# Moved loads, shorter transposes and grouped products in a two-layer trunk kernel

## The chip, the cores and the metric

The kernel runs on one core of a Trainium2 chip. The metric is the device time of one execution in microseconds (us); shown is the median of several runs. The core has TensorE (matrix products; its queue also holds the weight loads), VectorE, ScalarE, GpSimd and SyncE, which run side by side and wait for each other through semaphores. In the profile they are PE, PEld (weight loads), DVE, ACT, POOL and SP; SPq, ACTq and POOLq are the queues that issue DMA transfers.

## The reference

One sequence of 512 tokens of width 1024 passes two layers. Each layer has a token mixer, a cross attention to 256 memory vectors, and a feed-forward block with a short convolution; all sums go into the residual `h`. Layer 0 mixes with GLA and RWKV-7, layer 1 with RG-LRU and mLSTM.

```
mem_n = rms_norm(mem, mem_norm_g)
h = x
for layer in range(DEPTH):
    xn = rms_norm(h, norm_mix_g[layer])
    ...                      # layer 0: gla_group, rwkv7_group; layer 1: rglru_group, mlstm_group
    h = h + mixed @ w_mix_out[layer]
    h = h + memory_cross_attention(rms_norm(h, norm_xattn_g[layer]), mem_n, ...)
    h = h + conv_glu_ffn(rms_norm(h, norm_ffn_g[layer]), ...)
return rms_norm(h, final_norm_g)
```

GLA and RWKV-7 carry a state from chunk to chunk (64 tokens in the kernel): per chunk a state update from keys and values, and an output that reads the state before the chunk. Cross attention is a softmax over the 256 memory vectors in four heads.

## The kernel before

Activations lie transposed: eight tiles of 128 features x 512 tokens. A dense product is made of three TensorE products per 128 x 128 block: weights and activations are each split into a rounded part (`hi`, made on ScalarE) and the rest (`lo`, made on VectorE), and `hi*hi`, `hi*lo` and `lo*hi` are summed in PSUM. `wload` loads one block of weights on SP's queue into a ring of three raw tiles and splits it into a ring of two; `block` and `half` call it. PSUM has eight banks: a ring `mm` of three for dense products and a ring `ax` of five for all else. The pool `qr` has 16 tiles of 512 columns that serve many short-lived values.

The Tile framework orders the instructions: it goes by the order in which they are written and by what it reckons to be ready, so work written later fills gaps of work written earlier. On each engine that order is then fixed; an instruction that waits holds up all behind it on its engine. `issue_after(x)` puts instructions behind `x` on its engine. Products into one PSUM tile keep their written order.

The stages, with their times in the profile below:
- start (to 20 us): the constructor `Trunk` loads vectors and constants (`cmat`: identity, block ones, a mask) and runs ten small products on ones as warm-up; `trunk` loads the eight tiles of x and the first weights; the first loop in `gla` multiplies each x tile with the gate's low-rank weights (two products) and with the keys' weights (three).
- GLA (to about 88 us): projections, transposes, masked scores, then for two pairs of heads the sums `u` of keys and values of seven chunks and the state `S` from them, and the outputs.
- RWKV's four pairs (to about 232 us): per pair p the projections r, k, v, decays, v transposed into `SV`, products within chunks, and a bonus term that reads v last. `during(p)` puts GLA's gates and the memory's norm among them.
- RWKV's solve and scan (to about 340 us): a triangular inverse on VectorE, then eight chunks, each with products into `w`, `yp`, `z`, `uu` and again `yp`, for four pairs and two heads e of a pair. The two heads use different halves of the partitions; `SV[0]` is completed by VectorE, `SV[1]` by ScalarE. The products of the memory's keys and values (`memory_k`, `memory_v`), written later, run between.
- Cross attention: per head two halves of 256 tokens: scores, softmax `e`, transposes into `pT`, then values.
- Feed-forward, layer 1, and the end: the last block of `ffn` is done in two halves of 256 tokens, and `finish` adds, norms, scales and stores each half.

The state sums of GLA before, with one PSUM tile for two chunks each, written and read in turn:

```
for c in range(7):
    if c % 4 < 2:
        us[c // 4, c % 2] = K.ax.tile([P, 2, P], F32, name="ax")
    u = us[c // 4, c % 2][:, (c % 4) // 2]
```

Of the kernel before, what the change touches and what calls it, by code (L numbers as in the profile page):

```python
# [8 lines left out]
F32 = mybir.dt.float32  # L9
# [3 lines left out]
ALU = mybir.AluOpType  # L13
# [4 lines left out]
P = 128  # L18
# [124 lines left out]
class Trunk:  # L143
    def __init__(self, ctx, tc, I):
# [14 lines left out]
        nc.gpsimd.dma_start(out=self.cm, in_=I["cmat"][:, 0:384])  # L159
# [10 lines left out]
        for i in range(10):  # L170
            self.mmul(warm[:, 0:P], self.ones["d"], self.ones["d"])
# [6 lines left out]
        nc.vector.tensor_scalar(out=self.bo64m, in0=self.bo64, scalar1=1.0 / 64.0, scalar2=None, op0=ALU.mult)  # L178
# [61 lines left out]
    def wload(self, src, kb, m):  # L240
# [4 lines left out]
        n = kb * m  # L245
        self.last_load = nc.sync.dma_start(out=raw[:, :n], in_=src.rearrange("p k m -> p (k m)"))
        self.act(hi[:, :n], raw[:, :n], AF.Copy)
        self.tt(lo[:, :n], raw[:, :n], hi[:, :n].bitcast(F32), ALU.subtract)
        sh = lambda t: t[:, :n].rearrange("p (k m) -> p k m", m=m)
# [149 lines left out]
def xattn(K, l, nm, kd, vd, h, feed):  # L399
    nc, X = K.nc, nm.X  # L400
    with ExitStack() as es:
# [25 lines left out]
        def heads(hd, q):  # L427
            pT = [K.ax.tile([P, T], F32, name="ax") for _ in range(2)]
            for half in range(2):
# [18 lines left out]
                for i in range(2):  # L448
# [3 lines left out]
                    for m in range(2):  # L452
                        nc.tensor.transpose(pT[m][:, t * P:(t + 1) * P], e[:, i, m * P:(m + 1) * P], K.ident)  # L453
# [30 lines left out]
def memory_norm(K, sm):  # L484
# [5 lines left out]
    for i in range(4):  # L490
        f = K.qr.tile([P, T], F32, name="xs")
        nc.sync.dma_start(out=pair(f), in_=src[:, 2 * i:2 * i + 2])
        M.append(f)
        sq = K.qr.tile([P, T], F32, name="xs") if i else acc
# [7 lines left out]
    r = K.qr.tile([P, T], F32, name="xs")[:, 0:256]  # L502
# [90 lines left out]
def gla(K, nm, wga, wk, squares, after, Y):  # L593
    nc, X = K.nc, nm.X
    with ExitStack() as es:
# [5 lines left out]
        with K.tc.issue_after(after.ins):  # L601
            nc.vector.tensor_copy(out=gm, in_=gf)
        wa = gp.tile([48, 256], F32, name="walpha")
# [96 lines left out]
        for p in range(2):  # L700
            us = {}
            for c in range(7):
                if c % 4 < 2:
                    us[c // 4, c % 2] = K.ax.tile([P, 2, P], F32, name="ax")
                u = us[c // 4, c % 2][:, (c % 4) // 2]
                r = slice(64 * (c % 2), 64 * (c % 2) + 64)
                for e in range(2):
                    hd = 2 * p + e
                    K.mmul(u[64 * e:64 * e + 64], kt[p][r, c // 2, 64 * e:64 * e + 64],
                           v[r, c // 2, hd * P:(hd + 1) * P])  # L710
                if c == 0:
# [55 lines left out]
def rwkv(K, X, Y, during, after):  # L767
# [3 lines left out]
    with ExitStack() as core:  # L771
# [12 lines left out]
        with ExitStack() as es:  # L784
# [13 lines left out]
            vp = wt.tile([P, 640], F32, name="vp")  # L798
            nc.gpsimd.memset(vp, 0.0)
            for p in range(4):  # L800
                r = shifted(K, new(), K.block("w_rw", p, X), p, om)
                k = shifted(K, new(), K.block("w_rw", 4 + p, X), 4 + p, om)
                v = shifted(K, vp[:, 64:576], K.block("w_rw", 8 + p, X), 8 + p, om)
# [28 lines left out]
                for w0, w1 in ((0, 4), (4, 8), (8, 9)):  # L832
# [406 lines left out]
def trunk(tc, I, out):  # L1239
    nc = tc.nc  # L1240
    with ExitStack() as ctx:
        K = Trunk(ctx, tc, I)
        sm = K.pool(ctx, "nsm", 1)
        with ExitStack() as es:
# [8 lines left out]
            for k in range(1, KD):  # L1253
                load(k)
# [113 lines left out]
```

## Time and profile before

| | us |
|---|---|
| median of 3 runs (1559.96 to 1565.53) | 1561.15 |
| the profiled execution | 1558.83 |
| its span, first to last instruction | 1557.0 |
| TensorE busy in the span | 1527.6 |
| VectorE busy | 914.9 |
| ScalarE busy | 683.7 |
| GpSimd busy | 23.3 |

The span is what the profile shows; about 1.8 us of the execution lie outside it. Busy times say how much of the span an engine worked; an engine that is off the path loses nothing by idling. A product's duration includes its way through the array, so products overlap: the pace is read from one start to the next, not from durations.

### The profile page before, as it was taken

What the parts mean: (1) busy time and instruction counts of PE and PEld (TensorE: products, weight loads), DVE (VectorE), ACT (ScalarE), POOL (GpSimd) and SP (SyncE); (2) the same over time, 40 slices, a digit from 0 to 9 for tenths busy, and PEclk for the clock granted to TensorE, in tenths of its full rate; (3) what the DMA queues carried; (4) which work ended last, traced back from release to release, by engine and by line L of the source; (5) the groups of instructions that cost most, each with busy time, mean ns of one, the idle gap of its engine ahead of it and who ended that gap; (6) DMA issues with size and microseconds to landing.
All of it is one profiled execution on the core that took longest, in us unless ns stands there. A gap on an engine that the chain in (4) does not pass through costs nothing.

```text
span 1557.0 us, 20187 instructions
## 1 busy us (share of the span) xinstructions
PE 1527.6 (98%) x8077; PEld 1240.3 (80%) x8077; DVE 914.9 (59%) x1348; ACT 683.7 (44%) x1101; POOL 23.3 (1%) x62
## 2 busy tenths in 40 slices
PE   8999999999999999999999999999999999999997
PEld 6876777787888888888888878788888888888886
DVE  7537679645655755556633386777557556565333
ACT  5465563345444543333332267566345333333221
POOL 2000000001000000000000000000000000000000
PEclk9999999999999999999999999999999999999999
DMA  4222226226331333332233321224213333322332
GB/s 165 81 75 82 68 62 192 90 93 224 111 106 48 107 97 98 99 95 95 92 98 102 94 98 49 75 73 149 72 51 117 105 98 95 96 95 89 101 98 78
DMA packets 50175, 152.19 MB, mean 98 GB/s; under 512 B 5505, under 2 KB 8865, under 8 KB 50081
## 3 DMA queue, kind: packets, MB, share of 16 engines
q1 hardware_dynamic: 45664, 142.87, 29.2%
q10 hardware_dynamic: 3536, 5.38, 1.0%
q0 software_dynamic: 880, 2.66, 0.4%
q8 instruction: 63, 1.03, 0.3%
q14 instruction: 32, 0.25, 0.1%
HBM read 144.59 MB, written 6.29 MB: 97 GB/s over the span
## 4 chain that ended last, share of the span: by engine, by line
PE 89%; DVE 6%; ACT 3%; DMA 1%; issue 1%; SPq 0%; DVEq 0%; ACTq 0%
PE mm L209 77%; PE ax L209 10%; DVE wl L194 1%; ACT e L206 1%; PE ax L453 1%; ACT wh L206 1%; DVE tm L194 1%; DVE bb L892 0%; DVE tu L194 0%; DMA raw<-in_w_kv 0%; DMA raw<-in_w_gla 0%; DVE au L881 0%; DVE e L814 0%; ACT a L206 0%; DVE stk L203 0%
## 5 line engine op out<-in xcount | busy, mean ns | idle before, releaser
L209 PE MATMUL mm<-xs,wh 128*128 128x512 f32 (+1 forms) x3627 | 1110.4, 387 | 2.4 <-DVE vp L203 1.8
L209 PEld LDWEIGHTS mm<-xs,wh 128*128 128x128 f32 x3627 | 671.8, 188 | 147.9 <-issue 8.0
L209 PE MATMUL mm<-xs,wl 128*128 128x512 f32 (+1 forms) x1814 | 700.3, 386 | 0.6 <-DVE wl L194 0.5
L206 ACT ACTIVATE wh<-raw 128x1024 fp32r<-128x1024 f32 (+2 forms) x273 | 264.8, 970 | 528.5 <-PE mm L209 412.1
L194 DVE TENSOR_TENSOR wl<-raw,wh 128x1024 fp32r<-128x1024 f32 (+2 forms) x272 | 302.6, 1113 | 211.8 <-ACT wh L206 210.8
L209 PEld LDWEIGHTS mm<-xs,wl 128*128 128x128 f32 x1814 | 341.0, 188 | 71.9 <-issue 1.8
L194 DVE TENSOR_TENSOR upad<-mm,rstd 128x512 f32<-128x512 f32 (+1 forms) x52 | 35.9, 690 | 95.5 <-PE mm L209 95.3
L194 DVE TENSOR_TENSOR h<-h,mm 128x512 f32<-128x512 f32 (+1 forms) x73 | 49.5, 677 | 69.3 <-PE mm L209 69.1
L194 DVE TENSOR_TENSOR g<-mm,rstd 128x512 f32<-128x512 f32 (+1 forms) x44 | 30.4, 692 | 76.0 <-PE mm L209 75.9
L203 DVE SCALAR_TENSOR_TENSOR c<-upad,vec,c 128x512 f32<-128x512 f32 (+1 forms) x88 | 65.9, 749 | 3.3 <-ACT c L206 1.8
L209 PE MATMUL mm<-wh,xs 128*128 128x256 f32 (+1 forms) x256 | 66.4, 349 | 0.0
L206 ACT ACTIVATE c<-c 128x512 f32<-128x512 f32 (+1 forms) x44 | 27.8, 632 | 87.1 <-DVE c L203 87.1
L209 PEld LDWEIGHTS mm<-wh,xs 128*128 128x128 f32 x256 | 44.8, 194 | 6.3 <-issue 1.0
L209 PE MATMUL mm<-wl,xs 128*128 128x256 f32 (+1 forms) x128 | 45.3, 354 | 3.8 <-DVE wl L194 3.8
L206 ACT ACTIVATE xs<-g 128x512 fp32r<-128x512 f32 (+1 forms) x44 | 27.8, 633 | 26.9 <-DVE g L194 26.9
L206 ACT ACTIVATE c<-upad,vec 128x512 f32<-128x512 f32 (+1 forms) x44 | 35.3, 802 | 1.5 <-DVE upad L194 1.5
L206 ACT ACTIVATE e<-ax,mx,scl 128x256 f32<-128x256 f32 x32 | 17.8, 560 | 39.8 <-DVE mx L194 39.8
L194 DVE TENSOR_TENSOR g<-c,g 128x512 f32<-128x512 f32 (+1 forms) x44 | 30.4, 692 | 5.8 <-ACT c L206 1.4
L194 DVE TENSOR_TENSOR nacc<-nacc,nsq 128x512 f32<-128x512 f32 x45 | 32.8, 730 | 0.3
L203 DVE SCALAR_TENSOR_TENSOR xs<-h,vec,xs 128x512 fp32r<-128x512 f32 x40 | 29.9, 749 | 3.5 <-ACT xs L206 3.4
L194 DVE TENSOR_TENSOR xs<-ax,xs 128x512 fp32r<-128x512 f32 x32 | 21.3, 687 | 18.0 <-ACT xs L206 18.0
L206 ACT ACTIVATE xs<-h,vec 128x512 fp32r<-128x512 f32 x40 | 28.8, 719 | 6.5 <-DVE h L194 6.5
(353 smaller groups left out, 1221.9 us busy)
## 6 DMA issues: line engine op xcount, KB each, us to landing
raw<-in_w_up SPq DMA_DIRECT2D x86, 512.0 KB, 3.4
raw<-in_w_dn SPq DMA_DIRECT2D x32, 512.0 KB, 3.4
raw<-in_w_kk SPq DMA_DIRECT2D x16, 512.0 KB, 3.6
raw<-in_w_kv SPq DMA_DIRECT2D x16, 512.0 KB, 3.9
raw<-in_w_q SPq DMA_DIRECT2D x16, 512.0 KB, 3.6
raw<-in_w_o SPq DMA_DIRECT2D x32, 256.0 KB, 2.6
raw<-in_w_cd SPq DMA_DIRECT2D x16, 512.0 KB, 3.2
raw<-in_w_rw SPq DMA_DIRECT2D x14, 512.0 KB, 3.6
```

The costliest lines, as they stand in the source:

```text
L194: (eng or self.nc.vector).tensor_tensor(out=out, in0=a, in1=b, op=op)
L203: return self.nc.vector.scalar_tensor_tensor(out=out, in0=a, scalar=s, in1=b, op0=op0, op1=op1)
L206: return self.nc.scalar.activation(out=out, in_=a, func=f, **kw)
L209: self.last_mm = self.nc.tensor.matmul(out, lhsT=l, rhs=r, start=start, stop=stop)
L453: nc.tensor.transpose(pT[m][:, t * P:(t + 1) * P], e[:, i, m * P:(m + 1) * P], K.ident)
```

## The change

- Start: the constants are loaded on SP's queue behind all x tiles (before: first on GpSimd's queue), and the scaled block of ones made from them is computed later. `wload` can load and split a block in parts; the first block goes in two halves, with loads of x between. 16 warm-up products for 10.
- Attention: all eight transposes of a head follow its second half; `pT` is allocated there.
- The memory's norm loads on GpSimd's queue, and its squares lie in a one-buffer tile of RWKV's pool, not in `qr`.
- GLA: the sums of four chunks share a PSUM tile (one full bank); all products of a pair are written ahead of the first read.
- RWKV: v is a `qr` tile of its own without padding, with four transposes into one PSUM tile in place of nine in three.
- RWKV's scan: `w`, `uu` and the second products of `yp` are written with e=1 first, and the rest of each group is put behind its first product.
- End: the gain of the last norm is multiplied into `h[j]`, j < 7, on ScalarE ahead of time; `finish` then multiplies three blocks at once and stores 3 + 3 + 2 blocks.

```diff
@@ class Trunk
-        nc.gpsimd.dma_start(out=self.cm, in_=I["cmat"][:, 0:384])
...
-        for i in range(10):
+        for i in range(16):
             self.mmul(warm[:, 0:P], self.ones["d"], self.ones["d"])
...
-        nc.vector.tensor_scalar(out=self.bo64m, in0=self.bo64, scalar1=1.0 / 64.0, scalar2=None, op0=ALU.mult)
...
-    def wload(self, src, kb, m):
+    def wload(self, src, kb, m, parts=1, between=None):
...
+        n = kb * m // parts
+        src = src.rearrange("p k m -> p (k m)")
+        for i in range(parts):
+            s = slice(i * n, (i + 1) * n)
+            self.last_load = nc.sync.dma_start(out=raw[:, s], in_=src[:, s])
+            if between:
+                between(i)
+        for i in range(parts):
+            s = slice(i * n, (i + 1) * n)
+            self.act(hi[:, s], raw[:, s], AF.Copy)
+            self.tt(lo[:, s], raw[:, s], hi[:, s].bitcast(F32), ALU.subtract)
@@ xattn, heads
-            pT = [K.ax.tile([P, T], F32, name="ax") for _ in range(2)]
+            es = []
             for half in range(2):
...
-                    for m in range(2):
-                        nc.tensor.transpose(pT[m][:, t * P:(t + 1) * P], e[:, i, m * P:(m + 1) * P], K.ident)
+                    es.append(e[:, i])
+            pT = [K.ax.tile([P, T], F32, name="ax") for _ in range(2)]
+            for m in range(2):
+                for t in range(4):
+                    nc.tensor.transpose(pT[m][:, t * P:(t + 1) * P], es[t][:, m * P:(m + 1) * P], K.ident)
@@ memory_norm
-        nc.sync.dma_start(out=pair(f), in_=src[:, 2 * i:2 * i + 2])
+        nc.gpsimd.dma_start(out=pair(f), in_=src[:, 2 * i:2 * i + 2])
         M.append(f)
-        sq = K.qr.tile([P, T], F32, name="xs") if i else acc
+        sq = tmp.tile([P, T], F32, name="msq") if i else acc
...
-    r = K.qr.tile([P, T], F32, name="xs")[:, 0:256]
+    r = tmp.tile([P, T], F32, name="msq")[:, 0:256]
@@ gla
             nc.vector.tensor_copy(out=gm, in_=gf)
+            nc.vector.tensor_scalar(out=K.bo64m, in0=K.bo64, scalar1=1.0 / 64.0, scalar2=None, op0=ALU.mult)
...
-            us = {}
+            us = [K.ax.tile([P, 4, P], F32, name="ax") for _ in range(2)]
             for c in range(7):
-                if c % 4 < 2:
-                    us[c // 4, c % 2] = K.ax.tile([P, 2, P], F32, name="ax")
-                u = us[c // 4, c % 2][:, (c % 4) // 2]
+                u = us[c % 2][:, c // 2]
...
+            for c in range(7):
+                u = us[c % 2][:, c // 2]
                 if c == 0:
                     K.act(S[:, p, 0], u, AF.Copy)
@@ rwkv
-            vp = wt.tile([P, 640], F32, name="vp")
-            nc.gpsimd.memset(vp, 0.0)
...
-                v = shifted(K, vp[:, 64:576], K.block("w_rw", 8 + p, X), 8 + p, om)
+                v = shifted(K, new(), K.block("w_rw", 8 + p, X), 8 + p, om)
...
-                for w0, w1 in ((0, 4), (4, 8), (8, 9)):
-                    ps = K.ax.tile([P, 4, P], F32, name="ax")
-                    for w in range(w0, w1):
-                        nc.tensor.transpose(ps[:, w - w0], vp[:, w * 64:w * 64 + P], K.ident)
-                    if w0 < 8:
-                        K.act(SV[0][64:128, w0:w1, p], ps[64:128, :, 0:64], AF.Copy)
-                    w = max(w0, 1)
-                    K.act(SV[1][0:64, w - 1:w1 - 1, p], ps[0:64, w - w0:w1 - w0, 64:128], AF.Copy)
+                ps = K.ax.tile([P, 4, P], F32, name="ax")
+                for t in range(4):
+                    nc.tensor.transpose(ps[:, t], v[:, t * P:(t + 1) * P], K.ident)
+                for e in range(2):
+                    for i in range(2):
+                        K.act(SV[e][R[1 - e], i::2, p], ps[R[i], :, R[e]], AF.Copy)
...
-                during(p)
+                during(p, wt)
...
+            def group(products):
+                products[0]()
+                with K.tc.issue_after(K.last_mm.ins):
+                    for f in products[1:]:
+                        f()
...
-                for p in range(4):
-                    for e in range(2):
-                        K.mmul(w[R[e], p], stk[e][:, p, c, 0:64], SV[e][:, c, p])
+                group([lambda e=e, p=p: K.mmul(w[R[e], p], stk[e][:, p, c, 0:64], SV[e][:, c, p])
+                       for p in range(4) for e in (1, 0)])
...
+                    group([lambda e=e, p=p: K.mmul(uu[R[e], p], BKT[:, p, c, R[e]], SV[e][:, c, p])
+                           for p in range(4) for e in (1, 0)])
...
+                group([lambda e=e, p=p: K.mmul(yp[R[e], p], SV[e][R[e], c, p], BB[R[e], p, c, 64:128], False, p == 3)
+                       for p in range(4) for e in (1, 0)])
@@ trunk
-            wk = K.wload(I["w_gla"][:, 2], KD, P)
-            for k in range(1, KD):
+            rest = iter(range(1, KD))
+            wk = K.wload(I["w_gla"][:, 2], KD, P, 2, lambda i: load(next(rest)))
+            for k in rest:
                 load(k)
+            nc.sync.dma_start(out=K.cm, in_=I["cmat"][:, 0:384])
...
-        def during(p):
+        def during(p, tmp):
...
-                    for j in range(KD):
-                        K.stt(h[j][:, s], h[j][:, s], K.v("final_norm_g", j), r, ALU.mult, ALU.mult)
-                        if j % 2:
-                            (nc.sync, nc.scalar)[j // 2 % 2].dma_start(out=dst[:, j - 1:j + 1, s],
-                                                                      in_=ht[:, j - 1:j + 1, s])
+                    rb = r.rearrange("p (o m) -> p o m", o=1)
+                    for a, b in ((0, 3), (3, 6), (6, 8)):
+                        c = min(b, KD - 1)
+                        K.mul(ht[:, a:c, s], ht[:, a:c, s], rb.to_broadcast([P, c - a, 256]))
+                        if b > c:
+                            K.stt(h[c][:, s], h[c][:, s], K.v("final_norm_g", c), r, ALU.mult, ALU.mult)
+                        (nc.scalar if a == 3 else nc.sync).dma_start(out=dst[:, a:b, s], in_=ht[:, a:b, s])
+
+                def feed(j, t):
+                    nm.feed(j, t)
+                    K.act(t, t, AF.Copy, scale=K.v("final_norm_g", j))
```

## Rows read from the trace of the kernel before

**Rows 1.** The page's busy times; a piece of the chain of waits (start, length, what)

```profile
PE 1527.6 (98%) x8077; PEld 1240.3 (80%) x8077; DVE 914.9 (59%) x1348; ACT 683.7 (44%) x1101; POOL 23.3 (1%) x62
372.81 62.39 PE mm L209 x274
```

**Rows 2.** Windows of TensorE: stretch, length, busy (instructions), granted clock, DMA share, GB/s

```profile
0.00:20.00 20.00, 15.07 (x57) 0.91 0.74 261
300.00:320.00 20.00, 20.00 (x281) 1.00 0.34 105
```

**Rows 3.** Start: timeline, chain, one window (PE, PEld, DVE, ACT, POOL; third-last: clock)

```profile
2.23 4.64 PE L209 MATMUL mm<-ones_d 128*128 128x128 f32 x20 [2.23 <-POOL ones_d L166]
1.66 7.04 DMA raw<-in_w_gla
11.10 0.80 PE L209 MATMUL mm<-xs,wl 128*128 128x512 f32 x1 [0.52 <-DVE wl L194]
12.00:13.00 1.00, 1.00 (x4) 0.55 (x3) 1.00 (x3) 1.00 (x3) 0.00 (x0) 0.50 1.03 420
20.63 0.39 PE L209 MATMUL mm<-xs,wl 128*128 128x512 f32 x1
27.28 1.12 PE L209 MATMUL ax<-alr,walpha 48*128 48x512 f32 x2
```

**Rows 4.** Attention, first head: timeline of TensorE

```profile
452.17 0.39 PE L209 MATMUL mm<-xs,wl 128*128 128x512 f32 x1
452.50 0.70 PE L453 MATMUL ax<-cmat,e 128*128 128x128 f32 x4
452.96 0.48 PE L209 MATMUL ax<-khi,xs 128*128 128x256 f32 x2
```

**Rows 5.** One chunk of the scan: timeline of TensorE

```profile
314.28 0.28 PE L209 MATMUL mm<-xs,wh 128*128 128x256 f32 x1
314.49 0.33 PE L209 MATMUL ax<-sv,bkt 128*64 128x64 f32 x2
314.75 0.32 PE L209 MATMUL ax<-bb,sv 64*64 64x64 f32 x2
315.00 0.39 PE L209 MATMUL mm<-xs,wh 128*128 128x256 f32 x1
315.22 0.28 PE L209 MATMUL mm<-xs,wl 128*128 128x256 f32 x1
315.34 0.40 PE L209 MATMUL mm<-xs,wh 128*128 128x256 f32 x2
316.15 0.68 PE L209 MATMUL ax<-sv,bkt 128*64 128x64 f32 x14
...
318.50 0.33 PE L209 MATMUL ax<-sv,stk 128*64 128x64 f32 x2
318.67 0.28 PE L209 MATMUL ax<-stk,sv 128*64 128x64 f32 x2
```

**Rows 6.** GLA's state sums: timeline of TensorE

```profile
68.18 0.44 PE L209 MATMUL ax<-v,kt 64*64 64x128 f32 x4 [0.57 <-DVE sc L698]
71.03 1.13 PE L209 MATMUL ax<-v,kt 64*64 64x128 f32 x16
```

**Rows 7.** RWKV's pairs: timeline of TensorE

```profile
114.26 1.20 PE L835 MATMUL ax<-cmat,vp 128*128 128x128 f32 x9 [0.26 <-DVE vp L203]
140.44 0.73 PE L209 MATMUL mm<-xs,wh 128*128 128x512 f32 x2 [1.78 <-DVE vp L203]
```

**Rows 8.** The end: timeline of VectorE

```profile
1537.79 0.96 DVE L194 TENSOR_TENSOR wl<-raw,wh 128x768 fp32r<-128x768 f32 x1 [3.87 <-ACT wh L206]
1550.36 3.25 DVE L203 SCALAR_TENSOR_TENSOR h<-h,vec,nsq 128x256 f32<-128x256 f32 x8 [2.19 <-ACT nsq L206]
```

**Rows 9.** Memory norm's loads and the first use of its result: timeline

```profile
124.33 1.45 SPq L492 DMA_DIRECT2D xs<-in_memT  x3
245.74 3.62 PE L209 MATMUL mm<-xs,raw 128*128 128x256 f32 x16
```

More of the change, by code (lines that the diff above doesn't have):

```diff
@@ L244, in wload @@
         lo = self.wh.tile([P, 1024], F32R, name="wl")
[L245 to L249, printed above, removed]
+        n = kb * m // parts
[9 more added lines that the diff above has]
+            self.tt(lo[:, s], raw[:, s], hi[:, s].bitcast(F32), ALU.subtract)
+        sh = lambda t: t[:, :kb * m].rearrange("p (k m) -> p k m", m=m)
         return sh(hi), sh(lo)
@@ L481, in xattn, with memory_norm @@
             feed(j, h[j])
-def memory_norm(K, sm):
+def memory_norm(K, sm, tmp):
     nc = K.nc
@@ L935, in rwkv @@
                     uu = K.ax.tile([P, 4, 64], F32, name="ax")
-                    for p in range(4):
-                        for e in range(2):
-                            K.mmul(uu[R[e], p], BKT[:, p, c, R[e]], SV[e][:, c, p])
+                    group([lambda e=e, p=p: K.mmul(uu[R[e], p], BKT[:, p, c, R[e]], SV[e][:, c, p])
+                           for p in range(4) for e in (1, 0)])
                     t = st.tile([P, 4, 64], F32, name="t")
@@ L944, in rwkv @@
                     K.mul(S, t, sb.to_broadcast([P, 4, 64]), nc.gpsimd)
-                for p in range(4):
-                    for e in range(2):
-                        K.mmul(yp[R[e], p], SV[e][R[e], c, p], BB[R[e], p, c, 64:128], False, p == 3)
+                group([lambda e=e, p=p: K.mmul(yp[R[e], p], SV[e][R[e], c, p], BB[R[e], p, c, 64:128], False, p == 3)
+                       for p in range(4) for e in (1, 0)])
                 for p in range(4):
@@ L1279, in trunk @@
         M = []
-        def during(p):
+        def during(p, tmp):
             if p == 0:
-                M.append(memory_norm(K, sm))
+                M.append(memory_norm(K, sm, tmp))
                 next(M[0])
@@ L1345, in finish @@
                     K.act(r, r, AF.Exp, scale=-0.5)
-                    for j in range(KD):
-                        K.stt(h[j][:, s], h[j][:, s], K.v("final_norm_g", j), r, ALU.mult, ALU.mult)
-                        if j % 2:
-                            (nc.sync, nc.scalar)[j // 2 % 2].dma_start(out=dst[:, j - 1:j + 1, s],
-                                                                      in_=ht[:, j - 1:j + 1, s])
-                ffn(K, l, nf, h, nm.feed, finish)
+                    rb = r.rearrange("p (o m) -> p o m", o=1)
[8 more added lines that the diff above has]
+                    K.act(t, t, AF.Copy, scale=K.v("final_norm_g", j))
+                ffn(K, l, nf, h, feed, finish)
 def kernel(**inputs):
```

## The prediction

> **What bounds the kernel now.** I read four views, in this order. First the busy times: TensorE is busy for 98% of the span, VectorE for 59%, ScalarE for 44%, and in the long dense stretches one 512-column product follows another every 62.39 / 274 = 0.228 us [rows 1]. So nearly every us of TensorE time is a us of the kernel, and the other engines matter only where TensorE waits for them. Second the windows of 20 us: the first one has 4.93 us without a product, while the scan of RWKV (300 to 320 us) shows none at all [rows 2]. Third the waits of TensorE, taken stage by stage. Fourth, and most important here, the order of the instructions: a busy TensorE is not a TensorE at its pace. Where short products of one kind are cut into pieces between long products of another, starts lie further apart although no idle time is shown. The change mostly removes such pieces, so its gain has to be read from distances between starts.
>
> **The start: first weights in two halves, the constant matrix later, 16 warm-ups for 10.** Now the first whole weight block (512 KB) lands 1.66 + 7.04 = 8.70 us into the span; ScalarE and VectorE must split it, and the dense stream only begins at 11.10 [rows 3]. TensorE had been idle from the end of its warm-ups at 6.87, and its granted clock lies at the lower level (0.50, 1.2 GHz) in the window from 12 to 13 us [rows 3]. The first loop holds 40 products (8 blocks of x with five each), 9.1 us at the pace of rows 1; its last one starts at 20.63 [rows 3], so it ends as if it had begun at 20.86 - 9.1 = 11.75. After the change 256 KB are enough, and the 192 KB of constants no longer run beside them. They land at the latest with the whole block, at 8.70, and at the earliest after half its time, 1.66 + 3.5 = 5.2; I take 6, or 7.5 behind the split. What then decides is the end of the warm-ups: 32 records at (4.64 - 0.42) / 19 = 0.22 us give 2.23 + 7.1 = 9.3; if the last 12 run at the upper level (about half of that) 8.0. The stream begins near 9 without a gap, 2.7 us earlier. Not all of it stays: the product on the gate input at 27.28 [rows 3] waits for the norm, hence for all x blocks and their squares, and x still comes over the same queue. I let 0.7 of it go there. The first VectorE instruction, which waited for the constants, and its moved copy (one short operation) cost nothing where they go: VectorE is idle 41% of the time. **-2.0 us**, ends -3.2 and 0.
>
> **Attention: transposes once a head.** Between 452.17 and 452.96 stand one 512-column product and four transposes: 0.79 us, of which 0.23 is the product and 0.46 the four transposes from start to start, 0.115 each [rows 4]. The other 0.10 is the change from one kind to the other, and I take as much again for the way back. Eight heads lose one such pair each: 8 x 0.2 = **-1.6 us**, ends -2.5 (entries that also wait for the softmax) and -0.5. The second half's wait was the later one anyway. The first transposes come later, then eight run in a row, +0.46 us on the head's own chain; queries of the next head or the output projection cover that (in an uncovered head it would cost these 0.46 us).
>
> **RWKV's scan: groups of products kept together.** At 314.49 the update of the state has its first two records, at 314.75 the output its first two; at 315.00 long products resume, and the other 14 + 14 come at 316.15 [rows 5]. The reason: e=0 is ready first, e=1 only after ScalarE's copy, and products into one tile keep their order. The piece costs 0.51 us where four records inside a run cost at most 4 x 0.68 / 14 = 0.19; the entry takes 0.21 (314.28 to 314.49) and the exit 0.22 (315.00 to 315.22) where a product of that shape takes 0.12 (315.22 to 315.34) [rows 5]. Together 0.32 + 0.09 + 0.10 = 0.51 us. With e=1 first the piece can't start early, so seven chunks save 3.6 us. The group ahead of it (318.50, 318.67) is cut likewise, but only `w` is grouped, not the first half of `yp`, so I count just the 0.17 from 318.50 to 318.67, seven times: 1.2 [rows 5]. The last chunk adds 0.2. **-5.0 us**; ends -8 (the cut ahead of `w` goes too) and -2 (other pieces take its place). The group's first product now waits for ScalarE's copy, and everything behind it on TensorE's queue waits too; the 14 others waited for the same copy before.
>
> **GLA's state sums in whole banks.** The 56 records come in seven runs, from runs of 4 up to the run of 16 at 71.03, which takes 1.13 us, 0.07 each; one run waits 0.57 us for VectorE to free a bank [rows 6]. With two or three runs four or five cuts go, at the 0.2 of the scan: 0.9, and a part of the waits: **-1.2 us**. Ends -2.5 and +0.5. The loss: the reads begin only behind the 14th product of a pair. What speaks against it stands in the Trainium skill, page "PSUM — Partial Sum Buffer", section "Terms": two engines may not use the same bank and quadrant at once, so with both sums in whole banks no read can overlap a write. Were the output waiting for that, 24 records x 0.07 = 1.7 us later, the part would be +0.5 and the sum 1.7 us smaller; the trace agrees so far that a run of these products waits for VectorE.
>
> **RWKV's v without padding.** Four transposes take the place of nine in each of four pairs [rows 7]: 4 x 5 x 0.115 = 2.3 us of TensorE. And `vp` is one buffer, so the second pair's v must wait until the first pair's bonus has read it; TensorE stood 1.78 us for that at 140.44 [rows 7]. Now v has a tile of its own. The copies go from five to four on ScalarE, and two PSUM tiles a pair become free: not counted. **-4.1 us**, ends -6 and -1.5 (the wait moves to another operand).
>
> **The end.** Eight operations on VectorE (3.25 us) [rows 8] become two of 768 elements (0.96 each, as the subtraction of that size [rows 8]) and two of 256 (3.25 / 8 = 0.41): 2.74, less the overlap: **-0.6 us**, ends -0.9 and 0 (the last store queues behind larger ones). The seven scalings on ScalarE lie in a stage where it is mostly idle; if one held back a weight block, under 0.7 us once.
>
> **The memory norm on GpSimd's queue.** Four loads leave SP's queue, where three of them were issued at 124.33 [rows 9], and get in front of GpSimd's clearing of the next pair's first column. Nothing waits for it within tens of us; 0, with the loss below.
>
> **Sum:** 2.0 + 1.6 + 5.0 + 1.2 + 4.1 + 0.6 = 14.5 us. The profiled execution took 1558.83 us (span 1557.0), so 1544.3; it was 2.3 us under the median of the runs, 1561.15, and against that the forecast is **1546.5**.
>
> **Rivals.** (a) The groups don't stay together: the first half of `yp` and the long products cut them as before. For it: `yp` is not grouped, its e=0 is ready first [rows 5]. Then 1.5 of the 5 us come: 1550. Chance 0.13. (b) The freed TensorE time turns into waits: the scan and the solve ahead of it are chains over VectorE, and with less time lost TensorE runs out of long products in front of a wait. For it: VectorE is the next busiest [rows 1]; against it: no idle time in the scan, with long products between all groups [rows 2, 5]. Scan and RWKV give back most of their 9 us: 1554 to 1556. Chance 0.10. (c) More comes: the waits around the RWKV pairs go with the shorter ScalarE and PSUM queues, the start reaches 3.2, the scan 8: 1538. Chance 0.07. (d) Slower: the memory loads sit in GpSimd's queue behind an operation that waits for a later pair, so the normed memory is late and the products of the first `memory_k` on unsplit weights (8 blocks x 8, two records each), which now fill the solve stage at 3.62 / 16 = 0.23 us a record [rows 9], run behind it instead: 29 us more against 14.5 gained, 1576. It decides from about 100 us delay of the loads on (124.33 against the stream at 245.74, less the norm's own work). The Trainium skill, page "SBUF — State Buffer", section "SBUF: two separate sides", says that GpSimd can't write descriptors while VectorE holds their shared port; that alone would delay a load by single operations, not by 100 us. Chance 0.04. The forecast keeps 0.66.
>
> **How the numbers follow.** About 0.5% (7.8 us) is what a measurement can tell from no change. The forecast's own spread is 1541 to 1551.5. The range 1539 to 1555 adds (a), half of (b) and some of (c), and leaves out 0.15. Faster by over 0.5% (under 1553.3): the forecast, (a), (c) and none of (b), less a tail of the sum: 0.83. Slower: (d), 0.04. The same: 0.13.
>
> **What would show it.** The dense stream begins near 9 us with no granted clock at 0.50 behind it; no run of two records ahead of the 14s in the scan's updates; runs of eight transposes in attention and of four for v; no wait for v at the second pair; four operations at the end. It is wrong where TensorE shows new waits between 230 and 340 us, or where pieces of two records remain.

## The result and the profile after

| | before | after |
|---|---|---|
| median of the runs | 1560.56 us (1559.24 to 1565.53) | 1544.45 us (1543.66 to 1545.37) |
| profiled execution | 1558.83 us, span 1557.0 | 1545.02 us, span 1543.2 |

The ratio is 0.9887 with a 95% interval from 0.9865 to 0.9908: faster by 0.9 to 1.35%, 16.1 us by the medians. The forecast of 1546.5 lies 2 us above the median, and the range held it. The sum came out; several of its terms did not.

The page of the changed kernel, busy times (answers to [rows 1]): TensorE still sets the time.

```profile
PE 1518.2 (98%) x8069; PEld 1235.4 (80%) x8069; DVE 912.6 (59%) x1341; ACT 688.7 (45%) x1105; POOL 25.5 (2%) x64
```

Windows of the same execution (start:end, length, busy (instructions) of PE, PEld, DVE, ACT, POOL, then granted clock, DMA share, GB/s); the first two answer [rows 2, 3], the others show the solve stage ahead of RWKV's scan:

```profile
0.00:20.00 20.00, 18.52 (x87) 14.59 (x87) 13.01 (x18) 14.35 (x22) 8.57 (x25) 1.00 0.75 267
12.00:13.00 1.00, 1.00 (x6) 0.75 (x5) 1.00 (x3) 1.00 (x3) 0.00 (x0) 1.00 1.00 410
260.00:270.00 10.00, 8.13 (x215) 6.52 (x209) 7.95 (x6) 4.11 (x7) 0.00 (x0) 0.57 0.15 42
270.00:280.00 10.00, 10.00 (x134) 7.47 (x130) 3.96 (x7) 2.60 (x8) 0.70 (x1) 0.75 0.24 81
```

The clock of 0.50 at the start is not there; it shows in none of the nine profiles of this study with the new start, and in two of the five with the old one. In the solve stage the clock is 0.57 and 0.75 over 20 us. In the kernel before the clock falls in this stage too, but later and for a shorter time (its first product on au and bb is at 273.25):

```profile
270.00:280.00 10.00, 8.79 (x293) 6.97 (x293) 9.86 (x7) 6.04 (x9) 0.00 (x0) 1.00 0.32 105
280.00:290.00 10.00, 8.18 (x102) 5.92 (x98) 5.79 (x10) 1.73 (x7) 0.70 (x1) 0.83 0.35 107
```

Timeline of TensorE in the changed kernel, in the order of [rows 3, 6, 7, 5, 4]: warm-ups, first product with a weight block, product on the gate input; GLA's sums; a pair's v; the solve's first products; one chunk of the scan; attention.

```profile
1.00 5.90 PE L207 MATMUL mm<-ones_d 128*128 128x128 f32 x32 [1.00 <-POOL ones_d L165]
7.21 0.62 PE L207 MATMUL mm<-xs,wh 128*128 128x512 f32 x2
24.31 1.09 PE L207 MATMUL ax<-alr,walpha 48*128 48x512 f32 x2
...
64.08 0.44 PE L207 MATMUL ax<-v,kt 64*64 64x128 f32 x4
65.09 2.10 PE L207 MATMUL ax<-v,kt 64*64 64x128 f32 x52 [0.57 <-DVE sc L708]
67.12 1.16 PE L207 MATMUL ax<-sc,v 128*128 128x128 f32 x8
68.83 1.13 PE L207 MATMUL ax<-sc,v 128*128 128x128 f32 x8 [0.56 <-DVE S L201]
...
109.21 0.66 PE L842 MATMUL ax<-cmat,xs 128*128 128x128 f32 x4 [0.26 <-DVE xs L201]
...
258.91 2.09 PE L207 MATMUL ax<-au,bb 32*32 32x32 f32 x120 [1.41 <-DVE au L896]
262.87 0.42 PE L207 MATMUL ax<-au,bb 32*32 32x32 f32 x8 [1.87 <-issue]
...
301.89 0.69 PE L207 MATMUL ax<-sv,bkt 128*64 128x64 f32 x16
302.50 0.68 PE L207 MATMUL ax<-bb,sv 64*64 64x64 f32 x16
...
438.94 0.70 PE L462 MATMUL ax<-cmat,e 128*128 128x128 f32 x4
439.40 0.48 PE L207 MATMUL mm<-xs,wl 128*128 128x512 f32 x1
439.71 0.63 PE L207 MATMUL mm<-xs,wh 128*128 128x512 f32 x2
440.18 0.66 PE L462 MATMUL ax<-cmat,e 128*128 128x128 f32 x4
```

To see here: the warm-ups begin 1.23 us earlier; GLA's 56 records stand in two runs, not seven; v takes four transposes; the scan's groups are whole, without a run of two ahead; but attention still shows two runs of four, with three long products between them.

The end, VectorE (answers to [rows 8]): three products with the norm and one fused operation, 2.6 us instead of 3.25.

```profile
1537.10 2.16 DVE L192 TENSOR_TENSOR h<-h,nsq 128x768 f32<-128x768 f32 x3 [2.19 <-ACT nsq L204]
1539.18 0.48 DVE L201 SCALAR_TENSOR_TENSOR h<-h,vec,nsq 128x256 f32<-128x256 f32 x1
```

Where the 13.8 us between the two spans lie, by the distance of the same instructions in both traces (two names with a comma are the tiles that a product reads; wa,w2a2 stands as wa,w2a in the timelines):

| stretch | before | after | gain |
|---|---|---|---|
| to the product on the gate input | 27.28 | 24.31 | 2.97 |
| from GLA's first qd,ki to the first wa,w2a2 | 46.16 | 44.21 | 1.95 |
| RWKV's pairs (to the last xs,cmat) | 118.85 | 111.60 | 7.25 |
| to the first au,bb (solve, VectorE's chain) | 43.05 | 41.01 | 2.04 |
| to the first sv,stk (solve, products) | 6.04 | 10.41 | -4.37 |
| scan (to the last bb,sv) | 59.55 | 52.49 | 7.06 |
| to attention's first khi | 108.04 | 111.04 | -3.00 |
| attention with the feed-forward behind it: from the first khi to mLSTM's first product; in layer 1 to the last norm's product | 470.26, 451.33 | 470.34, 451.32 | -0.07 |
| mLSTM | 70.41 | 71.17 | -0.76 |
| from the last norm's product to the end | 8.34 | 7.79 | 0.55 |
| all else | | | 0.18 |

The pairs' 7.25 us have three parts. TensorE's waits there fall from 5.9 to 2.6 us, so 3.3 us. Twenty transposes fewer are 2.3 us by the prediction's price. The third part is a loan: 8 products fewer of the memory's keys stand among the pairs (26 records instead of 34, 0.23 us each: 1.8 us). The 3.00 us lost behind the scan are the other end of such loans: 23 long products more stand there (469 records instead of 446). From wa,w2a2 to khi it is 9.0 us, where the prediction had 9.1 (v and scan). mLSTM measures 70.4 to 71.2 us over all profiles of this study, whatever the kernel: scatter.

### The profile page after: what moved, and what is told of

The parts are those of the page before. It is cut to its first block, busy times and chain, and to the rows that moved or that the text cites. A ratio compares the mean times of both kernels' runs of the same rounds, so it can differ in the third digit from the quotient of the medians.

```text
span 1543.2 us, 20154 instructions
## 1 busy us (share of the span) xinstructions
PE 1518.2 (98%) x8069; PEld 1235.4 (80%) x8069; DVE 912.6 (59%) x1341; ACT 688.7 (45%) x1105; POOL 25.5 (2%) x64
## 4 chain that ended last, share of the span: by engine, by line
PE 87%; DVE 7%; ACT 3%; issue 2%; DMA 1%; POOL 0%; SPq 0%; DVEq 0%; ACTq 0%
PE mm L207 76%; PE ax L207 10%; DVE wl L192 1%; ACT wh L204 1%; PE ax L462 1%; DMA raw<-in_w_kv 0%; DVE tm L192 0%; ACT e L204 0%; DVE tu L192 0%; ACT xs L204 0%; DVE au L887 0%; DVE xs L192 0%; DMA x<-in_xT 0%; ACT a L204 0%; DVE stk L201 0%
## 5 line engine op out<-in xcount | busy, mean ns | idle before, releaser
L192 DVE TENSOR_TENSOR xs<-ax,xs 128x512 fp32r<-128x512 f32 (+1 forms) x36 | 24.0, 686 | 20.8 <-ACT xs L204 20.8
L192 DVE TENSOR_TENSOR xs<-g,xs 128x512 fp32r<-128x512 f32 (+1 forms) x44 | 30.1, 685 | 2.5 <-ACT xs L204 2.5
```

The costliest lines, as they stand in the source:

```text
L192: (eng or self.nc.vector).tensor_tensor(out=out, in0=a, in1=b, op=op)
```

## The experiments

In each comparison the ratio is against runs of the kernel before on the same chip. Times between executions of one kernel go with the mean granted clock: the kernel before took 1554.9 us in one with a mean of 0.999 and 1567.7 us in one with 0.987. So each part is read from its stretch of the trace first, and from the time second.

**The start alone** (kernel before with this part):

```diff
-        nc.gpsimd.dma_start(out=self.cm, in_=I["cmat"][:, 0:384])
...
-        for i in range(10):
+        for i in range(16):
...
+            wk = K.wload(I["w_gla"][:, 2], KD, P, 2, lambda i: load(next(rest)))
...
+            nc.sync.dma_start(out=K.cm, in_=I["cmat"][:, 0:384])
```

> The kernel before with the start's part alone: constants' load behind the x blocks on SP's queue, 16 warm-ups, first weight block in two halves, the scaled mask made later. Theory, from the trace after: the constants' load also stood ahead of the ones' memset, so the warm-ups begin at 1.0 instead of 2.23; the last product of the first loop comes near 16.3 instead of 20.63, of which about 3.0 us reach the product on the gate input (27.28 before) and stay: about 3.0 us less than the kernel before. The step as recorded: 2.0 us. Rival: the stages behind (GLA, RWKV's pairs, the solve stage) are bound by VectorE and ScalarE and take it back: under 0.7 us less.

Measured: the gate input's product at 24.38, 2.9 us earlier, as in the full change. The time shows none of it: 1563.06 us, ratio 1.0004 (0.9981 to 1.0026). Its executions fall into two groups: 1554.4 to 1557.4 us with a mean clock of 0.995 to 0.999, and 1563 to 1565 us with 0.989 or 0.990. At a mean clock of 0.999 one execution took 1554.57 us, and one of the kernel before on the same chip 1556.01: 1.4 us less. The profiled one is of the second group, and the windows show where (start_alone):

```profile
60.00:70.00 10.00, 9.26 (x97) 6.85 (x95) 5.51 (x12) 2.53 (x6) 0.00 (x0) 0.84 0.37 105
70.00:80.00 10.00, 10.00 (x61) 8.17 (x59) 1.97 (x7) 0.14 (x1) 0.00 (x0) 0.50 0.01 2
80.00:90.00 10.00, 10.00 (x57) 6.78 (x58) 1.38 (x2) 4.87 (x9) 0.00 (x0) 0.80 0.00 0
```

TensorE is busy throughout, but at 0.50 (1.2 GHz) from GLA's state sums on: 53.6 us from qd,ki to wa,w2a2 instead of 46.2. The rival, that VectorE and ScalarE bind the stages behind and take the gain back, is not what this profile shows; the low clock in GLA's stage covers the gain. Whether that fall is an accident or follows from the new start isn't shown. Four of the seven executions have a mean clock of 0.990 or less, against two of sixteen of the kernel before on this chip. And of the six profiles with GLA's sums as before, the two whose clock stays up in GLA's stage are the two in which it falls at the start instead: the kernel before [rows 3] and v_mem, a run that is shown further down:

```profile
12.00:13.00 1.00, 1.00 (x4) 0.59 (x3) 1.00 (x3) 1.00 (x2) 0.00 (x0) 0.50 1.01 404
```

**GLA's whole banks alone:**

```diff
-                if c % 4 < 2:
-                    us[c // 4, c % 2] = K.ax.tile([P, 2, P], F32, name="ax")
...
+            us = [K.ax.tile([P, 4, P], F32, name="ax") for _ in range(2)]
...
+            for c in range(7):
+                u = us[c % 2][:, c // 2]
...
```

> The kernel before with GLA's state sums in whole banks alone. The step as recorded: 1.2 us. Theory: two runs of v and kt instead of seven give 2.7 us of work (from the first product of qd and ki to the last of sq and ones_h), and beside that the stretch of half clock that stood at 66 to 88 us in the profiles of the start alone and of the scan alone (about 8 us lost in each) does not come, as it did not with whole banks in the changed kernel: no granted clock under 0.9 between 60 and 90 us, and no execution with a mean clock under 0.991. Rival: that stretch has nothing to do with the sums and comes by chance, then it is seen here too and the time is within 3 us of the kernel before.

Measured: 1556.21 us, ratio 0.9978 (0.9963 to 0.9994). The stretch takes 44.20 us for 46.16: 2.0 us, where the theory had 2.7. Its clock is 1.00 from 60 to 90 us, and ten executions lie between 1555.1 and 1557.7 us with mean clocks of 0.993 to 0.997.

**The changed kernel without GLA's part** (the same lines the other way round):

> The changed kernel with GLA's state sums as before (four half banks). Theory: the stretch from the first product of qd and ki to the first of wa and w2a2 takes 46.2 us instead of 44.2, and in about a quarter of the executions the clock falls to 0.50 in it for some 17 us, as in the profiles of the start alone and of the scan alone, which costs 8 us more: a median of 1546 to 1549 us, single executions up to 1556 us with a mean clock under 0.991. Rival: the low clock there belongs to other parts of the kernel before; then all executions lie within 3 us of 1546.5 us, and none has a mean clock under 0.992.

Measured: 1547.28 us, ratio 0.9926 (0.9903 to 0.9948). Four executions at 1543.2 to 1547.3 us (clock 0.993 or 0.994), two at 1553.6 and 1554.4 (0.988, 0.989). The profiled one is one of the two (no_gla, windows):

```profile
70.00:80.00 10.00, 10.00 (x59) 8.24 (x60) 1.52 (x5) 0.59 (x2) 0.00 (x0) 0.50 0.01 2
80.00:90.00 10.00, 10.00 (x62) 7.01 (x61) 1.56 (x3) 5.63 (x11) 0.00 (x0) 0.92 0.00 0
```

The theory held: the low clock came in two of six executions, where it had about a quarter. Over the whole study: of six profiles with half banks (the kernel before among them) four show 0.50 in GLA's stage, of eight with whole banks none. None of the 40 executions with whole banks has a mean clock under 0.992; with half banks five of 55 of the kernel before and 15 of 37 of the other kernels have 0.990 or less (a mean counts the falls of every stage, so this is a sign only). So the part is worth 2.0 us by the two profiles with half banks and no fall there, and where the fall would have come 3 to 8 us more (the stretch took 49.0, 52.1, 53.6 and 53.8 us in the four). It also takes away most of the scatter: gla_alone's ten executions lie within 2.6 us, the 21 of the kernel before on the same chip within 12.8. What in the cut sums brings the clock down isn't shown; in both forms TensorE waits about 0.6 us once or twice there.

**The scan's groups alone:**

```diff
+            def group(products):
+                products[0]()
+                with K.tc.issue_after(K.last_mm.ins):
+                    for f in products[1:]:
+                        f()
...
-                for p in range(4):
-                    for e in range(2):
-                        K.mmul(w[R[e], p], stk[e][:, p, c, 0:64], SV[e][:, c, p])
+                group([lambda e=e, p=p: K.mmul(w[R[e], p], stk[e][:, p, c, 0:64], SV[e][:, c, p])
+                       for p in range(4) for e in (1, 0)])
...
```

> The kernel before with the kept-together product groups of RWKV's scan alone. Theory, from the trace after: the cut ahead of the output's first half goes too, although it is not grouped, because the group ahead of it no longer begins with two records; the scan from the first product on sv and stk to the last on bb and sv takes 52.5 us instead of 59.6, and 7 us reach the end. The step as recorded: 5.0 us. Rival: a part of the 7 us in the trace after comes from the later place of long products (other parts of the change), then the scan alone takes 54 to 56 us and 3 to 5 us reach the end. Rival (b) of the prediction: waits take it back, under 2 us.

Measured: 1552.19 us, ratio 0.9952 (0.9929 to 0.9975), 7 us by the medians. The scan takes 53.3 us for 59.6, with groups of 16 throughout, those of the output's first half too; 0.4 us of waits for VectorE and five gaps of 0.12 us, for ScalarE's copy, come in their place. From wa,w2a2 to khi this profile shows 5.1 us only (330.4 for 335.5), because 1.05 are lost ahead of the solve stage's products, where the clock is at 0.50 for 6.9 us instead of 3.4.

**RWKV's v alone, and with the memory norm's part:**

```diff
-                v = shifted(K, vp[:, 64:576], K.block("w_rw", 8 + p, X), 8 + p, om)
+                v = shifted(K, new(), K.block("w_rw", 8 + p, X), 8 + p, om)
...
+                for t in range(4):
+                    nc.tensor.transpose(ps[:, t], v[:, t * P:(t + 1) * P], K.ident)
...
```

and in the second kernel also:

```diff
-        nc.sync.dma_start(out=pair(f), in_=src[:, 2 * i:2 * i + 2])
+        nc.gpsimd.dma_start(out=pair(f), in_=src[:, 2 * i:2 * i + 2])
...
-        sq = K.qr.tile([P, T], F32, name="xs") if i else acc
+        sq = tmp.tile([P, T], F32, name="msq") if i else acc
```

> The kernel before with RWKV's v without padding alone (four transposes a pair for nine, v in a tile of its own). Theory: five transposes fewer in each of four pairs and the wait for vp gone are worth about 6 us of the pairs' stage, but the pairs end earlier with fewer long products ahead, and in the solve stage TensorE runs dry and at half its clock for longer, which takes 4 us back: about 2 us less at the end. The step as recorded: 4.1 us less. Rival: the loss in the solve stage has to do with the other parts (the scan's groups, the loads on GpSimd's queue), then 5 to 6 us less at the end.

> The kernel before with two parts: RWKV's v without padding, and the memory norm with a tile of its own for the squares and its loads on GpSimd's queue. With the first part alone TensorE stood 5.7 us at 138 to 144 us: ScalarE's queue was held by a square that waited for a memory load issued late on SP's queue. Theory: the second part takes just this wait away, the 5.7 us and the half clock behind them go, and the two parts together give 4 to 6 us against the kernel before, and 9 us or more against the first part alone. Rival: the memory norm is beside the point (as the prediction had it, 0), the wait comes from v's use of the shared ring of 16 tiles, and a wait of over 3 us stays at the second pair.

Measured: alone it is slower, 1567.94 us, ratio 1.0052 (1.0037 to 1.0067); together faster, 1553.45 us, 0.9968 (0.9947 to 0.9989). Timeline of v alone, all engines:

```profile
134.32 0.95 SPq L492 DMA_DIRECT2D xs<-in_memT  x2
138.86 0.63 ACT L206 ACTIVATE xs<-xs 128x512 f32<-128x512 f32 x1 [0.78 <-DMA xs<-in_memT]
139.52 0.69 ACT L206 ACTIVATE e<-ax,neg 128x512 f32<-128x512 f32 x1
140.10 0.68 ACT L206 ACTIVATE a<-ax,neg 128x512 f32<-128x512 f32 x1
140.67 0.72 ACT L206 ACTIVATE e<-e,col_one 128x512 f32<-128x512 f32 x1
141.28 0.71 ACT L206 ACTIVATE a<-a,col_one 128x512 f32<-128x512 f32 x1
141.90 0.62 ACT L206 ACTIVATE xs<-xs 128x512 f32<-128x512 f32 x1
142.41 1.83 ACT L206 ACTIVATE xs<-mm,om 128x512 f32<-128x512 f32 x3
143.16 2.06 DVE L203 SCALAR_TENSOR_TENSOR xs<-mm,vec,xs 128x511 f32<-128x511 f32 x3
143.96 1.22 PE L209 MATMUL mm<-xs,wh 128*128 128x512 f32 x2 [5.68 <-DVE xs L203]
```

With v in the shared ring of 16 tiles the last two memory loads are issued at 134.32; in the kernel before three were issued at 124.33 [rows 9] and only the last late. Now the three shifted copies of the next pair (142.41) stand on ScalarE's queue behind the two squares that need these loads. ScalarE itself is idle for a load for only 0.78 us; the rest is order: four operations on the gates (139.52 to 141.28) stand between the two squares and so ahead of the copies too. TensorE stops for 5.68 us, and the clock is 0.51 over the 10 us behind 140. (Of this profile's loss 2.8 us are the fall in GLA's stage.) With the second part the loads are issued from 121.57 on and the squares don't hold the ring:

```profile
121.57 2.94 POOL L492 DMA_DIRECT2D xs<-in_memT  x4 [0.39 <-issue]
135.90 1.13 PE L209 MATMUL ax<-wa,w2a 64*128 64x512 f32 x4
```

The pairs take 111.6 us instead of 118.9 (119.9 with v alone), and from wa,w2a2 to khi 331.0 instead of 335.5: 4.5 us (start_alone and gla_alone, which have the pairs as before, take 337.3 and 336.9 there, so a us or two is scatter). The theory held in the time, and the wait is gone; which of the two, tile or queue, does it, these runs don't separate.

**Eight transposes kept in a row**, in the changed kernel:

```diff
-            for m in range(2):
-                for t in range(4):
...
+            first = turn(0, 3)
+            with K.tc.issue_after(first.ins):
+                for m, t in ((0, 2), (0, 1), (0, 0), (1, 3), (1, 2), (1, 1), (1, 0)):
+                    turn(m, t)
```

> The changed kernel, with the eight transposes of a head ordered directly behind one another; in the changed kernel itself three long products still stand between two runs of four. Theory: a cut costs about 0.2 us, as the prediction had it, and eight cuts go: 1.6 us less than the changed kernel, about 13.4 + 1.6 us less than the kernel before after rounding the profiled times, so 15.5 us. Rival: the first transposes now wait for the second half's softmax, so the long products between come ahead instead and nothing is gained: the same as the changed kernel, 13.8 us less than before; or the wait of the eight for the softmax shows as idle time, up to 0.5 us a head more.

Measured: 1542.73 us, ratio 0.9896 (0.9881 to 0.9911). The two stretches from attention's first khi, with the feed-forward, take 469.82 and 450.87 us for 470.34 and 451.32 in the changed kernel, 0.5 each, and three further kernels with this edit give the same within 0.06. So a cut costs 0.12 us here, not 0.2, and the edit is worth 1.0 us; the time, 1.7 us under the changed kernel's, agrees but can't tell it alone.

```profile
439.33 1.10 PE L460 MATMUL ax<-cmat,e 128*128 128x128 f32 x8
```

**Ten warm-ups, and the first block whole**, in the changed kernel:

```diff
-        for i in range(16):
+        for i in range(10):
```

and in the other kernel instead:

```diff
-            wk = K.wload(I["w_gla"][:, 2], KD, P, 2, lambda i: load(next(rest)))
+            wk = K.wload(I["w_gla"][:, 2], KD, P, 1, lambda i: load(next(rest)))
```

> The changed kernel with 10 warm-ups instead of 16. Theory: the warm-ups begin at 1.0 us and end near 5.6, the first weights are split at 6.6, so a gap of about 1 us opens and nothing else: the clock was not the lower one before the first products anyway, and the time is that of the changed kernel within 0.5 us (about 14 us less than the kernel before). Rival (as the prediction argued): after a gap the granted clock falls to 0.50 within the first loop and 2 to 4 us are lost, 1547 to 1549 us.

> The changed kernel with the first weight block loaded and split whole (one load, one split), all else of the start as changed. Theory: the halves carry the start's gain: the first product with a weight block comes at 9 to 10 us instead of 7.21, and the product on the gate input 1 to 2 us later than 24.3. Rival: behind the first block the x blocks set the pace (TensorE waited 0.47 us for one at 8.53, and the norm's sum for GpSimd's adds at 22 us), so the gate input's product comes within 0.5 us of 24.3, and the earlier constants and ones carry the gain.

Measured: with ten, 1543.27 us, ratio 0.9893 (0.9857 to 0.9929), the gate input's product at 24.49 and the clock 1.00 from 0 to 20 us: the six more warm-ups do nothing. With the whole block 1545.83 us, ratio 0.9904 (0.9869 to 0.9938), and that product at 25.50: the halves carry 1.2 us (the eight profiles with halves lie at 23.98 to 24.73). Timeline of whole_block, the two waits that the halves avoid:

```profile
8.43 0.73 PE L207 MATMUL mm<-xs,wh 128*128 128x512 f32 x2 [0.65 <-ACT wh L204]
9.69 0.50 PE L207 MATMUL mm<-xs,wl 128*128 128x512 f32 x1 [0.53 <-DVE wl L192]
```

**Covering the idle time of the solve stage**, three kernels on top of the eight transposes:

```diff
+            spare = K.ax.tile([P, T], F32, name="ax")
+            for i in range(4):
+                K.mmul(spare[:, 0:256], K.ones["d"], flat(Tt)[:, 768:1024])
```

The first has five such products more, on flat(Tt)[:, 64:320]; the third has these four and, in memory_v, the products on wl behind all those on wh.

> The changed kernel with the eight transposes in a row (1542.7 us on this chip) and nine products more in the solve stage, whose sums nobody reads: five of 256 columns ahead of the first idle time there, four ahead of the products on au and bb, 0.46 us each, 4.1 us in all. They cover idle time of TensorE (2.4 and 1.4 us). Theory: the half clock from 260 to 274 us follows from the idle times ahead of it and the small products in it; with the idle times covered the clock stays up and 4 to 6 us come back: 1537 to 1539 us. Rival: the clock falls by the small products themselves or by the stop in the middle of them, which the added ones do not cover: 1542 to 1544 us, and the clock still 0.5 there.

> The changed kernel with the eight transposes in a row and four products more, whose sum nobody reads, ahead of the products on au and bb only (the idle time of 1.6 us there is covered by 2.0 us of work; the five products that waited for VectorE are left out). Theory: the clock falls there because the engine first stands idle and then runs 32x32 products; with the cover it stays up until after the solve stage, and 3 to 5 us come back: 1538 to 1540 us, and the first product on sv and stk comes at 265 us instead of 269. Rival: the clock falls in the 32x32 products all the same, or the gain goes into the next wait (for ws): 1542 to 1544 us.

> As the one with the cover, and in the memory's value products those on the low halves of a weight block come behind those on its high half, so that VectorE's subtraction has eight long products (1.8 us) instead of two (0.46 us) of time. Theory: the waits of 2.4 and 0.65 us for the low half shrink by up to 1.4 and 0.65 us: 1 to 2 us less than with the cover alone. Rival: the end of the solve stage is set by VectorE's own chain of 62 short operations, so TensorE only waits later: no difference.

Measured: 1546.09 us, 0.9905 (0.9875 to 0.9935); 1542.41 us, 0.9887 (0.9872 to 0.9902); 1542.15 us, 0.9880 (0.9862 to 0.9899). By the ratios none can be told from the eight transposes alone, and neither the 1537 to 1540 us of the first two theories nor the 1 to 2 us of the third came. The first is rather slower: from wa,w2a2 to khi it takes 328.3 us, with the eight transposes alone 326.0. Windows of solve_fill, then of cover:

```profile
260.00:270.00 10.00, 7.43 (x253) 6.18 (x248) 8.63 (x8) 5.77 (x9) 0.00 (x0) 0.94 0.12 26
270.00:280.00 10.00, 9.91 (x130) 7.22 (x130) 4.31 (x9) 3.65 (x10) 0.80 (x2) 0.89 0.36 118
```

```profile
260.00:270.00 10.00, 8.37 (x228) 6.94 (x222) 8.27 (x7) 4.70 (x8) 0.00 (x0) 0.72 0.17 46
270.00:280.00 10.00, 9.91 (x145) 7.61 (x146) 4.46 (x9) 2.27 (x7) 0.73 (x2) 0.94 0.21 70
```

The clock does stay higher (0.94 and 0.72 for 0.57 in the changed kernel), and the scan begins at 265.05 and 267.28 instead of 268.96 with the eight transposes alone. In solve_fill the five early products came ahead of the memory's and waited 3.18 us for VectorE, a slip of mine. In both the long products that the added ones displace come behind the scan (from its end to khi 117.1 and 113.9 us, with the eight transposes alone 111.2), so what is won ahead is paid there. In cover the wait ahead of the 32x32 products goes but the stop in the middle of them stays (1.63 us), and the clock falls 2 us behind it. Neither decides alone: in all fourteen profiles the clock falls to 0.50 in this stage, between 1 and 11 us behind the first product on au and bb, and in gla_alone, where there is no such stop, it does so after 3 us. What sets the moment, and what the low clock alone costs here, stays open. That the cover or the order of the products gives anything to the total can't be told.

## Why the prediction was right, and where it was not

| term | predicted | in the two traces | part alone, by its stretch |
|---|---|---|---|
| start | 2.0 (3.2 to 0) | 3.0 | 2.9 |
| attention | 1.6 (2.5 to 0.5) | 0 | 1.0 where they do stand in a row |
| scan | 5.0 (8 to 2) | 7.1 | 6.3 |
| GLA | 1.2 (2.5 to -0.5) | 2.0 | 2.0, and no low clock |
| v | 4.1 (6 to 1.5) | 1.9 (9.0 from wa,w2a2 to khi, less the scan) | slower alone; 4.5 with the memory's part |
| end | 0.6 | 0.6 | not run |
| memory norm | 0 | see v | |

**The start** was right in size, wrong in its reason. I had the end of 16 warm-ups decide; ten give the same. The step that failed is "what then decides is the end of the warm-ups". On GpSimd's queue the constants' load stood ahead of the clearing of the ones; without it the warm-ups begin at 1.00 instead of 2.23 and are over at 6.90, ahead of the first product with a weight block (7.21). The halves give about 1.2. The rest goes with the clock: the profiled execution before had 0.50 at 12 to 13 us [rows 3] and v_mem too (gate input at 26.88), but the three other profiles with the old start did not and reach it at 25.4 to 26.1; against those the gain is 1 to 2 us. That the new start keeps the clock up was argued, not tested by itself.

**Attention** failed at the step "eight run in a row". Writing them one behind the other does not keep them there: the first half's four are ready earlier and are put where they are ready. "0.2 a pair", taken from one distance [rows 4], was also twice the 0.12 that an edit that does keep them gave.

**The scan** was right in its mechanism. The term was mis-sized because I let the cut ahead of the output's first half stay; it went, since the group ahead of it no longer starts with a run of two. Rival (a) is refuted, and so is rival (b) in the scan. The 7.1 of the two traces are no clean measure: they hold a wait of 1.8 us for ws (before, at 282.92) that is not there after, and 5.7 us at the low clock instead of 3.4; the part alone gives 6.3.

**GLA** was mis-sized by 0.8. The price I set against it is there, and small: the second set of sc,v products waits 0.56 us for VectorE's work on S (line at 68.83), where I had put 1.7. The rule that I weighed, that two engines may not use one bank and quadrant at once (the Trainium skill, page "PSUM — Partial Sum Buffer", section "Terms"), sets no price, and no run here shows whether this wait comes from it; the stretch is 2.0 us shorter all the same. Nor did the trace before bear it out: the run that waits in [rows 6] waits for VectorE's work on the scores sc, and does so for 0.57 us in both forms.

**v and the memory norm**: the size was right for the two together, the bookkeeping was not. The waits that went are 3.3 us and not the 1.78 of one row. "Nothing waits for it within tens of us; 0" was read from a trace in which v did not use the ring. Once v takes a tile there, the way the memory's squares and loads are placed decides whether the pairs gain 7 us or lose 1. I had named the end of the range, "the wait moves to another operand", and not seen that another part of the change holds it off.

**Rival (b)** came true in part, at the solve stage that it names, but not in its way. The solve stage's products took 4.4 us longer, and yet the waits did not grow: from 228 to 300 us TensorE's waits sum to 6.0 us after and 6.2 before. What grew is the time at 0.50, some 17 us in this window instead of 7, with one stop of 1.87 us that no wait explains. With it v brings 1.9 instead of 4.1. The sign "new waits between 230 and 340 us" showed here, and "runs of eight transposes in attention" did not. The other signs came, but for waits of up to 0.4 us of the transposes for v.

**Rival (d)** did not come: the memory's four loads are issued on GpSimd's queue within 3 us, and the first product on the normed memory follows at 207.6 us (216.8 before).

```profile
116.86 2.93 POOL L501 DMA_DIRECT2D xs<-in_memT  x4 [0.39 <-issue]
```

The sum of 14.5 against 13.8 in the traces is a balance: scan 2.1, start 1.0 and GLA 0.8 more, v 2.2, attention 1.7 and mLSTM 0.8 less, 0.2 elsewhere.

## What to carry to other kernels

Price an edit by the distance of the same instructions in two traces, not by its total: here a part worth 2.9 us of its stretch could not be seen in times that move by 10 us with the granted clock. An edit that takes a buffer from a shared ring has to be read together with everything else that uses the ring or stands on the same engine's queue; a part that was priced at nothing may be what makes another pay. If products are to stay together, tie them to the one that is ready last; their order in the source does not do it.

## What the runs showed of the hardware

- TensorE's granted clock falls to 0.50 without any idle time of length: in GLA's stage it did so in four of six profiles behind many short runs of 64x64 products with two waits of 0.2 to 0.6 us, and in none of eight with the same products in two runs and two waits of 0.6 us. One such fall cost 3 to 8 us.
- In the nine profiles in which stores of the memory's values and a weight load overlap the solve's 32x32 products (DMA share 0.79 to 1.01 in the first us of these), TensorE stops there or right behind for 0.8 to 2.0 us and waits for nothing that the profile shows; in the five others (0.53 to 0.67) it does not. That the transfers are the cause was not tested, and they are over when the stop begins, as in the changed kernel:

```profile
259.90:260.90 1.00, 1.00 (x69) 0.99 (x63) 0.97 (x2) 0.73 (x2) 0.00 (x0) 1.00 0.38 137
260.90:261.90 1.00, 0.10 (x7) 0.00 (x0) 1.00 (x1) 0.45 (x1) 0.00 (x0) 0.73 0.00 0
```

A rival that wasn't tested is that TensorE waits for its own instructions: on q8, the queue of kind "instruction" in the profile, a packet of 16 KB starts 1.2 to 1.8 us behind the first of these products in the nine, and 2.1 to 2.6 us behind it in the five.
